# Where one branch of the first gate tile is projected: in the gate stage, or among the last attention blocks

## The chip, the cores and the metric

The kernel runs on one core of a Trainium2 chip. The core has a matrix engine (TensorE, PE in the profile, with its weight loads as PEld), a vector engine (VectorE, DVE), a scalar engine (ScalarE, ACT), a general engine (GpSimd, POOL) and a queue that issues most DMAs (SyncE, SP). Each engine works through its own instructions in order and waits on semaphores for the others. The metric is the device time of one execution in microseconds (us), with all inputs in device memory.

## The reference

One decoder block over a sequence of 1024 tokens of width 1024. A row norm is followed by a wide projection `w_in`; its columns give a forgetting attention (8 heads of 64), a differential attention (4 heads with two maps of 64 each), a SiLU factor z for both, and 2 x 1024 gate columns.

```python
h = rms_norm(x, g_pre[l], NORM_EPS)
proj = jnp.einsum('bsd,dn->bsn', h, w_in[l])
qa, ka, va, fa, za, qb, kb, vb, zb, gates = jnp.split(proj, SPLIT_POINTS, axis=-1)
...
ya = merge_heads(ya) * jax.nn.silu(za)
...
yb = merge_heads(yb) * jax.nn.silu(zb)
gate_a, gate_b = jnp.split(jax.nn.sigmoid(gates), N_BRANCHES, axis=-1)
merged = (gate_a * jnp.einsum('bsw,wd->bsd', ya, w_branch[l, 0])
          + gate_b * jnp.einsum('bsw,wd->bsd', yb, w_branch[l, 1]))
y = jnp.einsum('bsd,de->bse', merged, w_out[l])
x = x + rms_norm(y, g_post[l], NORM_EPS)
```

## The kernel before

All matrix operands are float32, cut in a high part (cast to float32r) and a low part (the difference). A product of two such operands is three matmuls: high by high, high by low, low by high. So each weight tile needs two instructions before PE can use it (`load_w`, L277): one for `hi`, one for `lo`; its arguments choose the engines.

The work goes in stages. First the transposed, normed input h^T is made (`hT`, 8 buffers) and the values are projected. Then come eight attention units, `u` = 0 to 7 (L642): 0 to 3 differential, 4 to 7 forgetting. While unit u attends, PE is given "filler": the q and k projections of unit u + 1 and some z projections, whose results are stored to device memory (`spill_tasks`, L383: load a weight tile, then two chunks of 512 tokens, 24 matmuls each into `ps`, copied by ACT to `zs` and stored). Unit 7 has no next unit; its filler is z6 and z7 alone.

A forgetting unit has two heads, m = 0 and 1, and takes 256 query rows at a time, block g = 3 down to 0. For each (g, m): scores (`s_row`, tiles Sf, two matmuls per piece), a minimum and bias on DVE, the exponential on ACT, a reciprocal on DVE and a scaling on POOL. The products of the block before are made meanwhile (`av`, L464): PE transposes 128 x 128 pieces of the softmax rows into a PSUM tile (`ptf`, L481, two buffers), ACT casts it (`phf`, L484), DVE subtracts (`plf`, L485), PE multiplies with V into one PSUM tile (`ypf`, L505, one buffer), and ACT and DVE take it out (`yt` L587, `ys` L588) for a store to `y_d`. The loop L661 to L673 emits, for each of the eight blocks n of a unit, its scores, then the products of the block before, then the filler that is due. The order on each engine is not the order in which the code is written: a scheduler sets it with a timeline of its own, within the dependences.

The gate stage (L802 to L850) makes gate tile d = 0 with the plain product (`gates_plain`: both branches, two chunks each, 96 matmuls, `pg`), and tiles d = 1 to 7 in pairs of branches with seven products in place of eight (`gates_pair`, `wino`, tiles x_g; 12 matmuls each). The seven products are numbered 1 to 7; 1, 2 and 3 use h^T itself, 4, 6, 5 and 7 use combinations of h^T that were stored earlier and are loaded here as eight tiles of 1 MB (`h_load`, T4 to T7, in buffers that attention held). The left operands a1 to a7 come from the two raw weight tiles by sums on POOL (S1 to S4) and a split on ACT and DVE or POOL, and take the buffers of `hi` and `lo` in turn with a third pair. `GATE` (L842) is the order of the products. Gates go through a sigmoid on ACT and are stored in `g_d`. `y_load` loads attention's results, `y_work` multiplies them by SiLU(z); `YORD` says after which tile.

Then y is cast to y^T (`yT`, high on ACT, low on DVE, L867 and L868), the branch products follow (`branch`, tiles pb, weights `br` by `load_w` with the high part on ACT and the low part on POOL, L899), each multiplied by its gate (`merge`), and the output product with its norm ends the kernel.

Of the kernel before, what the change touches and what calls it, by code (L numbers as in the profile page):

```python
# [32 lines left out]
        ((0, 0), (0, 1), (1, 0)), ((1, 1), (2, 0), (2, 1)), ((3, 0), (3, 1)), ())  # L33
ZFILL = ((0,), (1,), (), (2,), (3,), (4,), (5,), (6, 7))
# [13 lines left out]
def tile_hybrid_block(  # L48
# [58 lines left out]
    g_d = [[dram.tile([P, S], F32, name=f"g_d{d}_{b}") for b in range(2)] for d in range(KT)]  # L107
    ss_d = dram.tile([4, S], F32, name="ss_d")
# [194 lines left out]
    with ExitStack() as st:  # L303
# [135 lines left out]
        lastx, vload = [None], []  # L439

        def s_row(T, m, i, X, bias, boff, nm, le=None):

            A, B = (T["TA"], T["KA"]) if m == 0 else (T["TB"], T["KB"])
            n = (i + 1) * P
            qs = slice(i * P, (i + 1) * P)
            xs = slice(i % 2 * P, (i % 2 + 1) * P)
            pr = pp.tile([P, S], F32, tag="P", name=f"P{nm}_{m}_{i}")
            mx = small.tile([P, 2], F32, tag="mx", name=f"mx{nm}_{m}_{i}", bufs=8)
            pcs = pieces(i)
            for j, (a, b) in enumerate(pcs):  # L450
                ps = sps.tile([P, CH], F32, tag="S", name=f"S{nm}_{m}_{i}_{j}")[:, 0:b - a]
                nc.tensor.matmul(ps, lhsT=A[:, qs], rhs=B[:, a:b], start=True, stop=False)  # L452
                nc.tensor.matmul(ps, lhsT=X[:, xs], rhs=B[:, a:b], start=False, stop=True)  # L453
                nc.vector.tensor_tensor_reduce(  # L454
                    out=pr[:, a:b], in0=ps, in1=bias[:, boff + a:boff + b], scale=-0.125,
                    scalar=BIG if j == 0 else mx[:, j - 1:j], op0=ALU.add, op1=ALU.min,
                    accum_out=mx[:, j:j + 1])
            if le is None:
                le = small.tile([P, 1], F32, tag="l", name=f"l{nm}_{m}_{i}", bufs=8)
            nc.scalar.activation(pr[:, 0:n], pr[:, 0:n], AF.Exp,  # L460
                                 bias=mx[:, len(pcs) - 1:len(pcs)], scale=-1.0, accum_out=le)
            return pr, le
# [173 lines left out]

        T, tasks = unit_proj(0)
# [4 lines left out]
        for u in range(8):  # L642
# [18 lines left out]
            for n, (wgt, rws, prd) in enumerate(groups):  # L661
# [9 lines left out]
                while nf < len(fill) and nf < len(fill) * done / total:  # L671
                    fill[nf]()
                    nf += 1  # L673
        pend()
# [108 lines left out]
    def y_load(t):  # L783

        g = t // 2
        if t % 2 == 0:
# [22 lines left out]
    def gates_plain(d):  # L809
        for br in range(2):  # L810
            wt = load_w(f"g{br}_{d}", w_cols(GT + br * D + d * P), True, True)
            for c in range(2):
# [7 lines left out]

    def h_load():
# [3 lines left out]
        for m in (4, 6, 5, 7):  # L825
            for part in range(2):
                nc.sync.dma_start(f32(ts[m][part]), t_d[m][:, part])
            h_ops[m] = [[t[:, k, :] for k in range(4)] for t in ts[m]]

    def gates_pair(d, order):  # L830
        raw = []
        for br in range(2):
            r = wpool.tile([P, KT, P], F32, tag="wraw", name=f"raw{d}_{br}")
            nc.sync.dma_start(r, w_cols(GT + br * D + d * P))
            raw.append(r)
# [6 lines left out]
    GATE = (1, 2, 4, 6, 5, 7, 3)  # L842
    h_load()
    gates_plain(0)
    for t in (4, 5, 6, 7, 0, 1, 2, 3):
        y_load(t)
    for d in range(1, KT):
        gates_pair(d, GATE if d < KT - 1 else (7, 5, 6, 4, 1, 2, 3))
# [13 lines left out]

    yT = {}
# [32 lines left out]
    for br in range(2):  # L896
        for d in range(KT):
            if d % 2 == 0:
                wbr = load_w(f"br{br}_{d}", None, True, True, [  # L899
                    (slice(4 * n, 4 * n + 4),  # L900
                     wb[br][:, (d + n) * P:(d + n + 1) * P].rearrange("(k p) n -> p k n", p=P))
                    for n in range(2)])
# [178 lines left out]
```

## Time and profile before

| | us |
|---|---|
| median of three runs | 911.37 (909.87 to 914.45) |
| the profiled execution | 909.96 |
| its span, first to last instruction | 908.1 |
| PE busy in the span | 884.7 |
| mean granted clock of PE | 0.998 of full |

The span is what the profile's columns of time count in; the 1.9 us between the span and the execution's own time lie around it. A row of a group reads: line, engine, operation, output and input names, shape, count, then busy time and mean length, then the idle time ahead of it and who ended it. A row of the timeline starts with the start and the length in us. The unit boundaries in this execution: the scores and blocks of unit 7 end at 579.75, the plain gate projections run from there to 601.6, the pairs of gate tiles to 736.3, then the branches.

### The profile page before, as it was taken

What the parts mean: (1) busy time and instruction counts of PE and PEld (TensorE: products, weight loads), DVE (VectorE), ACT (ScalarE), POOL (GpSimd) and SP (SyncE); (2) the same over time, 40 slices, a digit from 0 to 9 for tenths busy, and PEclk for the clock granted to TensorE, in tenths of its full rate; (3) what the DMA queues carried; (4) which work ended last, traced back from release to release, by engine and by line L of the source; (5) the groups of instructions that cost most, each with busy time, mean ns of one, the idle gap of its engine ahead of it and who ended that gap; (6) DMA issues with size and microseconds to landing.
All of it is one profiled execution on the core that took longest, in us unless ns stands there. A gap on an engine that the chain in (4) does not pass through costs nothing.

```text
span 908.1 us, 13652 instructions
## 1 busy us (share of the span) xinstructions
PE 884.7 (97%) x4600; PEld 746.4 (82%) x4600; DVE 606.3 (67%) x1133; ACT 441.6 (49%) x877; POOL 447.2 (49%) x429
## 2 busy tenths in 40 slices
PE   7999999999999999999999999999999999999996
PEld 5899988788888888888888887788888888888885
DVE  6767547878678575467648548415678895648796
ACT  3433226576658584365545648534444352314352
POOL 7325325546555455254434446418566532483961
PEclk9999999999999999999999999999999999999999
DMA  9556747434335260432523432496555599210495
GB/s 323 188 177 255 270 119 194 110 82 130 102 87 163 70 180 18 147 86 71 165 74 84 133 100 65 180 402 224 160 162 186 176 308 327 71 46 0 122 198 168
DMA packets 128648, 139.04 MB, mean 153 GB/s; under 512 B 10289, under 2 KB 96305, under 8 KB 127554
## 3 DMA queue, kind: packets, MB, share of 16 engines
q1 hardware_dynamic: 124210, 135.82, 47.6%
q0 software_dynamic: 4224, 2.10, 2.0%
q8 instruction: 36, 0.59, 0.3%
q14 instruction: 34, 0.28, 0.1%
q10 hardware_dynamic: 144, 0.26, 0.1%
HBM read 85.65 MB, written 37.81 MB: 136 GB/s over the span
## 4 chain that ended last, share of the span: by engine, by line
PE 82%; DVE 6%; issue 4%; POOL 3%; DMA 2%; ACT 2%; SPq 1%; POOLq 0%; DVEq 0%; ACTq 0%
PE x_g L744 15%; PE pb L878 10%; PE pv L197 9%; PE x_o L744 9%; PE pz L298 8%; PE pk L298 7%; PE pq L298 7%; PE ypf L505 3%; PE ptf L481 2%; PE pg L298 2%; PE ypd L505 2%; PE Sd L452 2%; PE ptd L481 1%; PE Sf L452 1%; PE Sd L453 1%
## 5 line engine op out<-in xcount | busy, mean ns | idle before, releaser
L197 PE MATMUL pv<-wvhi,hT 128*128 128x264 f32 (+2 forms) x384 | 88.8, 323 | 0.4 <-DVE hT L183 0.4
L298 PE MATMUL pz<-hT,hi_z 128*128 128x512 f32 x256 | 83.3, 397 | 0.2 <-ACT sq L410 0.2
L298 PE MATMUL pk<-hT,hi_k 128*128 128x512 f32 x256 | 82.3, 395 | 0.9 <-DVE KB L351 0.9
L298 PE MATMUL pq<-hT,hi_q 128*128 128x512 f32 x256 | 81.7, 393 | 0.0
L878 PE MATMUL pb<-yT,hi_br 128*128 128x512 f32 x256 | 78.4, 389 | 0.0
L744 PE MATMUL x_g<-T,a_g 128*128 128x512 f32 x336 | 78.1, 391 | 0.0
L744 PE MATMUL x_o<-wo_op,a_o 128*128 128x512 f32 x336 | 77.6, 392 | 0.0
L744 PEld LDWEIGHTS x_o<-wo_op,a_o 128*128 128x128 f32 x336 | 63.0, 188 | 14.5 <-DVE a_o L694 0.5
L744 PEld LDWEIGHTS x_g<-T,a_g 128*128 128x128 f32 x336 | 63.1, 188 | 13.9
L197 PEld LDWEIGHTS pv<-wvhi,hT 128*128 128x128 f32 x384 | 64.2, 189 | 6.1 <-DVE hT L183 0.7
L460 ACT ACTIVATE Pd<-Pd,mxd 128x128 f32<-128x128 f32 (+7 forms) x64 | 49.7, 777 | 35.5 <-DVE mxd L454 35.1
L197 PE MATMUL pv<-wvlo,hT 128*128 128x512 f32 (+2 forms) x192 | 62.0, 325 | 0.7 <-DVE wvlo L153 0.7
L573 POOL TENSOR_TENSOR cb<-cb,trim 128x128 f32<-128x128 f32 x64 | 30.3, 477 | 65.7 <-DVE mxf L454 44.1
L485 DVE TENSOR_TENSOR plf<-ptf,phf 128x512 fp32r<-128x512 f32 (+1 forms) x80 | 50.0, 635 | 18.1 <-ACT phf L484 17.2
L547 POOL TENSOR_SCALAR Pd<-Pd,l,nlam 128x128 f32<-128x128 f32 (+7 forms) x32 | 29.3, 916 | 66.4 <-DVE l L546 60.2
L578 POOL TENSOR_SCALAR Pf<-Pf,lf 128x1024 f32<-128x1024 f32 (+3 forms) x64 | 47.9, 753 | 27.6 <-DVE lf L577 24.5
L460 ACT ACTIVATE Pf<-Pf,mxf 128x1024 f32<-128x1024 f32 (+3 forms) x64 | 49.9, 779 | 20.5 <-DVE mxf L454 19.7
L744 PE MATMUL x_g<-hT,a_g 128*128 128x512 f32 x252 | 59.0, 391 | 0.0
L878 PEld LDWEIGHTS pb<-yT,hi_br 128*128 128x128 f32 x256 | 48.0, 188 | 9.9
L744 PEld LDWEIGHTS x_g<-hT,a_g 128*128 128x128 f32 x252 | 47.3, 188 | 10.4
L298 PEld LDWEIGHTS pk<-hT,hi_k 128*128 128x128 f32 x256 | 47.2, 188 | 10.3 <-DVE KB L351 1.5
L298 PEld LDWEIGHTS pq<-hT,hi_q 128*128 128x128 f32 x256 | 47.6, 188 | 9.2
(253 smaller groups left out, 2366.1 us busy)
## 6 DMA issues: line engine op xcount, KB each, us to landing
t_d<-t SPq DMA_DIRECT2D x16, 512.0 KB, 4.2
T<-t_d SPq DMA_DIRECT2D x8, 1024.0 KB, 17.7
raw<-in_w_in_dram SPq DMA_DIRECT2D x14, 512.0 KB, 5.2
vb_d<-vbs SPq DMA_DIRECT2D x8, 512.0 KB, 3.8
va_d<-vas SPq DMA_DIRECT2D x8, 512.0 KB, 5.2
raw_k<-in_w_in_dram SPq DMA_DIRECT2D x8, 512.0 KB, 4.5
raw_q<-in_w_in_dram SPq DMA_DIRECT2D x8, 512.0 KB, 4.3
V<-vb_d SPq DMA_DIRECT2D x4, 1024.0 KB
```

The costliest lines, as they stand in the source:

```text
L197: nc.tensor.matmul(ps[n], lhsT=hT[hp][k // 4][i // 4][:, k % 4, hs], rhs=wt[k][:, a:b], start=first, stop=(k == KT - 1 and hp == 1))
L298: nc.tensor.matmul(ps, lhsT=a[:, k, :], rhs=hT[h][k // 4][c][:, k % 4, :], start=(k == 0 and a is hi and h == 0), stop=(k == KT - 1 and a ...
L452: nc.tensor.matmul(ps, lhsT=A[:, qs], rhs=B[:, a:b], start=True, stop=False)
L460: nc.scalar.activation(pr[:, 0:n], pr[:, 0:n], AF.Exp, bias=mx[:, len(pcs) - 1:len(pcs)], scale=-1.0, accum_out=le)
L481: nc.tensor.transpose(pt[:, o * P:(o + 1) * P], rows[2 * g + r][:, j * P:(j + 1) * P], ident)
L485: nc.vector.tensor_tensor(pl[:, 0:n], pt[:, 0:n], ph[:, 0:n], op=ALU.subtract)
L505: nc.tensor.matmul(o, lhsT=a, rhs=b[:, src], start=(j == 0 and n == 0), stop=(odd == 1 and jj == g and n == len(prods) - 1))
L547: nc.gpsimd.tensor_scalar(p2[:, 0:n], p2[:, 0:n], l2, nlam, op0=ALU.mult, op1=ALU.mult)
L573: nc.gpsimd.tensor_tensor(diag, diag, trim, op=ALU.add)
L578: nc.gpsimd.tensor_scalar(p1[:, 0:n], p1[:, 0:n], l1, 1.0, op0=ALU.mult, op1=ALU.mult)
L744: nc.tensor.matmul(x[m], lhsT=a[:, ai, k, :], rhs=right[m][bi][k], start=(k == 0 and n == 0), stop=(k == 3 and n == 2))
L878: nc.tensor.matmul(ps, lhsT=a[:, kk, :], rhs=yT[g][h][:, k % 2, sl], start=(k == 0 and a is hi and h == 0), stop=(k == 3 and a is lo))
```

## The change

It has five parts.

1. The first branch of gate tile 0 becomes a spilled projection, `gate`, of the form that z has: its weights are split on POOL and DVE, its two chunks are emitted in unit 7 after blocks n = 5 and n = 7 (`GFILL`), each behind the last score matmul of that block (`issue_after` orders it there on PE; `lasts` is that matmul), and stored to `gl_d`. `gates_plain` keeps the second branch alone, 48 matmuls in place of 96. After pair d = 2 the stored projection is loaded, goes through the sigmoid and is stored with the other gates.
2. The weights of the second branch are loaded ahead of the eight loads of T, and the raw weights of pair 1 are issued behind T4 in the code.
3. Pair 1 takes the products in the order 1, 2, 3, 4, 6, 5, 7: first those that need no T.
4. The loads of y are no longer issued together behind the plain projections, but each ahead of the pair after which it is used, behind that pair's raw weights on SP.
5. The first branch weight tile (`first`) is emitted ahead of the casts of y^T.

```diff
+GFILL = (5, 7)
...
-                nc.tensor.matmul(ps, lhsT=X[:, xs], rhs=B[:, a:b], start=False, stop=True)
+                lasts[0] = nc.tensor.matmul(
+                    ps, lhsT=X[:, xs], rhs=B[:, a:b], start=False, stop=True).ins
...
+        gate = spill_tasks("gl", GT, gl_d)
         T, tasks = unit_proj(0)
...
                     fill[nf]()
                     nf += 1
+                if u == 7 and n in GFILL:
+                    with tc.issue_after(lasts[0]):
+                        gate[GFILL.index(n)]()
...
     def gates_plain(d):
-        for br in range(2):
+        for br in (1,):
             wt = load_w(f"g{br}_{d}", w_cols(GT + br * D + d * P), True, True)
+            yield
...
+    def gate_raw(d):
+        raws[d] = []
+        for br in range(2):
+            r = wpool.tile([P, KT, P], F32, tag="wraw", name=f"raw{d}_{br}")
+            lastraw[0] = nc.sync.dma_start(r, w_cols(GT + br * D + d * P)).ins
+            raws[d].append(r)
...
+            if m == 4:
+                gate_raw(1)
...
+    plain = gates_plain(0)
+    next(plain)
     h_load()
-    gates_plain(0)
-    for t in (4, 5, 6, 7, 0, 1, 2, 3):
-        y_load(t)
+    run_all(plain)
     for d in range(1, KT):
-        gates_pair(d, GATE if d < KT - 1 else (7, 5, 6, 4, 1, 2, 3))
+        if d not in raws:
+            gate_raw(d)
+        with tc.issue_after(lastraw[0]):
+            for t, c in YORD[d]:
+                if c == 0:
+                    y_load(t)
+        gates_pair(d, (1, 2, 3, 4, 6, 5, 7) if d == 1 else GATE if d < KT - 1 else (7, 5, 6, 4, 1, 2, 3))
+        if d == 2:
+            for c in range(2):
+                g = tmp.tile([P, CH], F32, tag="t", name=f"g0_0_{c}")
+                nc.sync.dma_start(g, gl_d[:, c * CH:(c + 1) * CH])
+                gate_out(0, 0, c, g, g)
...
+    first = branch_w(0, 0)
     yT = {}
...
-                wbr = load_w(f"br{br}_{d}", None, True, True, [
-                    (slice(4 * n, 4 * n + 4),
-                     wb[br][:, (d + n) * P:(d + n + 1) * P].rearrange("(k p) n -> p k n", p=P))
-                    for n in range(2)])
+                wbr = first if br == d == 0 else branch_w(br, d)
```

On PE, near the end of unit 7 before, at the last scores (block 0 of head 1, Sf_1_0) and the transposes and products of blocks 2 and 1 (the digits after the name are head, block and piece, then a buffer number):

```order
L453 MATMUL Sf_1_0_0_6713<-KB_5341,X1f_0_6697 128x128
L505 MATMUL ypf_1_2_6515<-plf_1_2_2_6540,V_5848 128x256
L505 MATMUL ypf_1_2_6515<-phf_1_2_2_6539,V_5848 128x128
L505 MATMUL ypf_1_2_6515<-plf_1_2_2_6540,V_5848 128x128
L481 MATMUL ptf_0_1_1_6621<-ident,Pf_0_2_6505 128x128
```

The same place in the changed kernel (pgl is the moved projection; of a row of its matmuls the first ones are shown):

```order
L455 MATMUL Sf_1_0_0_6748<-KB_5342,X1f_0_6732 128x128
L300 MATMUL pgl_6773<-hT_91,hi_gl 128x512
L300 MATMUL pgl_6773<-hT_95,hi_gl 128x512
L300 MATMUL pgl_6773<-hT_91,lo_gl 128x512
...
L508 MATMUL ypf_1_2_6516<-plf_1_2_2_6541,V_5849 128x256
L508 MATMUL ypf_1_2_6516<-phf_1_2_2_6540,V_5849 128x128
L508 MATMUL ypf_1_2_6516<-plf_1_2_2_6541,V_5849 128x128
L484 MATMUL ptf_0_1_1_6622<-ident,Pf_0_2_6506 128x128
```

Between the last scores and the products that followed them stand 15 of the second chunk's 24 matmuls; 3 and 6 more stand behind the next two groups of transposes, and the last of them directly ahead of the first product of block 1. The first chunk stands likewise, 19 and 5, behind the scores of head 1's block 1 and behind the next two groups of transposes of head 0's block 2; the group of transposes ptf_1_2_2 (head 1, block 2) has none between it and those ahead of it.

On ACT, before, the end of unit 7 (yt takes a product out, phf casts a transposed block, the ACTIVATE is an exponential):

```order
L460 ACTIVATE Pf_1_0_6711,lf_1_0_6717<-Pf_1_0_6711,mxf_1_0_6712 128x128
L587 COPY yt_0_1_6638<-ypf_0_1_6611 64x256
L484 CAST phf_1_1_1_6677<-ptf_1_1_1_6676 128x384
L484 CAST phf_0_0_0_6723<-ptf_0_0_0_6722 128x384
L587 COPY yt_1_1_6692<-ypf_1_1_6666 64x256
```

And in the changed kernel (a_g are the left operands a1 and a2 of pair 1, sgl is the copy of the second chunk):

```order
L463 ACTIVATE Pf_1_0_6746,lf_1_0_6752<-Pf_1_0_6746,mxf_1_0_6747 128x128
L700 CAST a_g_6926<-raw_0_6858 128x512
L395 COPY sgl_6798<-pgl_6773 128x512
L700 CAST a_g_6944<-raw_0_6858 128x512
L590 COPY yt_0_1_6639<-ypf_0_1_6612 64x256
L487 CAST phf_1_1_1_6712<-ptf_1_1_1_6711 128x384
```

The two casts and the copy now stand between the last exponential and the copy yt; before, the casts of pair 1 stood behind the last phf of the unit and later.

On ACT at the passage to the branches, in the changed kernel; before, the cast of hi_br stood behind the two rows of yT from yf:

```order
L809 ACTIVATE zs_1_7906<-zs_1_7906 128x512
L286 CAST hi_br_0_8066<-raw_br_0_8063 128x1024
L900 CAST yT_2_8070<-yf_6924 128x1024 x2
L900 CAST yT_3_8076<-yf_7082 128x1024 x2
L754 COPY c_g_8004<-x_g_7991 128x512
```

More of the change, by code (lines that the diff above doesn't have):

```diff
@@ L107, in tile_hybrid_block @@
     g_d = [[dram.tile([P, S], F32, name=f"g_d{d}_{b}") for b in range(2)] for d in range(KT)]
+    gl_d = dram.tile([P, S], F32, name="gl_d")
     ss_d = dram.tile([4, S], F32, name="ss_d")
@@ L437, in swapped @@
             return t
-        lastx, vload = [None], []
+        lastx, vload, lasts = [None], [], [None]
         def s_row(T, m, i, X, bias, boff, nm, le=None):
@@ L785, in y_load @@
         g = t // 2
-        if t % 2 == 0:
+        if g not in yz:
             if t < 4:
@@ L819, in tile_hybrid_block @@
              for m, (kh, sh) in hB.items()}
+    raws, lastraw = {}, [None]
+    def gate_raw(d):
[4 more added lines that the diff above has]
+            raws[d].append(r)
     def h_load():
@@ L827, in h_load @@
                 nc.sync.dma_start(f32(ts[m][part]), t_d[m][:, part])
+            if m == 4:
+                gate_raw(1)
             h_ops[m] = [[t[:, k, :] for k in range(4)] for t in ts[m]]
     def gates_pair(d, order):
[L831 to L835, printed above, removed]
+        raw = raws[d]
         left = left_operands(f"g{d}", raw[0][:, 0:4], raw[0][:, 4:8], raw[1][:, 0:4], raw[1][:, 4:8])
@@ L861, in slot, with branch_w @@
         return s[0].tile(shape, dtype, tag=s[1], name=name)
+    def branch_w(br, d):
+        return load_w(f"br{br}_{d}", None, True, True, [
+            (slice(4 * n, 4 * n + 4),
+             wb[br][:, (d + n) * P:(d + n + 1) * P].rearrange("(k p) n -> p k n", p=P))
+            for n in range(2)])
+    first = branch_w(0, 0)
     yT = {}
```

## The prediction

> **What bounds it now.** The page comes first: which engine is full over the whole span.
>
> ```profile
> span 908.1 us, 13652 instructions
> PE 884.7 (97%) x4600; PEld 746.4 (82%) x4600; DVE 606.3 (67%) x1133; ACT 441.6 (49%) x877; POOL 447.2 (49%) x429
> ```
>
> PE (TensorE) is busy for 884.7 of 908.1 us. The change leaves PE's matmuls as many as they were, so it can win only from time in which PE stands still, and that is 23.4 us by this row. Next, busy time by stretch shows where: a piece of unit 7, the end of unit 7 cut in three, the plain gate projections, the first pair of gate tiles, the passage from gates to branches.
>
> ```profile
> core 0: us, PE busy (x) PEld busy (x) DVE busy (x) ACT busy (x) POOL busy (x), PEclk, DMA share, GB/s
> 528.90:549.00 20.10, 20.10 (x113) 17.27 (x111) 10.35 (x31) 11.62 (x23) 8.30 (x12) 1.00 0.34 106
> 549.00:563.41 14.41, 13.79 (x96) 11.76 (x95) 12.56 (x39) 11.44 (x24) 10.12 (x13) 1.00 0.27 75
> 563.41:574.37 10.96, 8.93 (x66) 7.41 (x65) 8.72 (x29) 8.85 (x25) 5.30 (x11) 1.00 0.04 13
> 574.37:579.75 5.38, 4.70 (x33) 3.92 (x34) 3.99 (x12) 4.18 (x12) 2.63 (x5) 1.00 0.12 38
> 579.75:601.60 21.85, 21.85 (x98) 18.07 (x98) 2.54 (x4) 5.11 (x9) 6.10 (x5) 1.00 0.99 395
> 601.60:620.60 19.00, 19.00 (x85) 15.59 (x83) 7.15 (x10) 6.47 (x11) 7.57 (x6) 1.00 1.04 378
> 725.00:750.00 25.00, 25.00 (x112) 20.61 (x111) 23.93 (x23) 14.03 (x18) 8.18 (x4) 1.00 0.93 313
> ```
>
> Until 549 the filler of unit 7 (the z projections) keeps PE full; from 601.60 on it is full too, also at the passage at 725 to 750. The hole is between 549 and 579.75, once the filler is used up and only softmax blocks are left. The waits of PE from 545 to 580 say for whom:
>
> ```profile
> PE ptf L481 <- DVE plf L485: 1.7, 4, 0.7
> PE ypf L505 <- DVE plf L485: 0.7, 3, 0.3
> PE ypf L505 <- ACT phf L484: 0.3, 1, 0.3
> PE ypf L505 <- DVE ys L588: 0.2, 1, 0.2
> ```
>
> Every one is a link of one block's chain: PE transposes a softmax block (pt), ACT casts it (ph), DVE takes the rest (pl), PE multiplies (yp), ACT and DVE take out the product (yt, ys). In 563.41 to 574.37 DVE and ACT are busy for 8.72 and 8.85 of 10.96 us, so neither is full; PE waits for their delay, not for their throughput, and other PE work in the gap would hide it.
>
> **How much PE stands still.** The busy column counts each matmul's modelled end, so I also go by starts. Two neighbours, a wait, and the marks of the last stretch, in PE's timeline:
>
> ```profile
> 565.82 0.28 PE L505 MATMUL ypf<-plf,V 128*128 128x256 f32 x1
> 565.94 0.28 PE L505 MATMUL ypf<-phf,V 128*128 128x256 f32 x1
> ...
> 568.24 0.62 PE L481 MATMUL ptf<-ident,Pf 128*128 128x128 f32 x4
> 568.62 0.36 PE L452 MATMUL Sf<-KB,TB 128*128 128x256 f32 x1
> 568.82 0.28 PE L453 MATMUL Sf<-KB,X1f 128*128 128x256 f32 x1
> 569.81 0.55 PE L481 MATMUL ptf<-ident,Pf 128*128 128x128 f32 x3 [0.71 <-DVE plf L485]
> ...
> 574.37 0.39 PE L505 MATMUL ypf<-phf,V 128*128 128x256 f32 x1
> ...
> 576.54 0.38 PE L505 MATMUL ypf<-phf,V 128*128 128x256 f32 x1
> ```
>
> A product of 256 columns takes 0.12 us from start to start, four transposes take 0.38, so 0.095 each. The groups of that window by line give what stands in 563.41 to 579.75:
>
> ```profile
> L505 PE MATMUL ypf<-plf,V 128*128 128x256 f32 (+1 forms) x26 | 6.8, 301 | 0.4 <-DVE plf L485 0.4
> L505 PE MATMUL ypf<-phf,V 128*128 128x256 f32 (+1 forms) x25 | 6.6, 288 | 0.7 <-ACT phf L484 0.3 <-DVE ys L588 0.2
> L481 PE MATMUL ptf<-ident,Pf 128*128 128x128 f32 x38 | 6.2, 280 | 1.6 <-DVE plf L485 1.5
> ```
>
> That is 51 products and 38 transposes; with the 9 score matmuls, 60 x 0.12 + 38 x 0.095 = 10.8 us of work in 16.34 us: 5.5 us of stall by starts, against (10.96 - 8.93) + (5.38 - 4.70) = 2.7 us by the busy column. The starts count what a filler could use, so I go by 5.5 and keep 2.7 as the low end. The last stretch holds 33 of the 98, 24 x 0.12 + 9 x 0.095 = 3.7 us of work, so 1.7 us of the stall lies there and 3.8 us ahead of it.
>
> **The change, part by part.**
>
> *The 48 matmuls that move.* The plain stretch holds 96 of them in 21.85 us, 0.228 each: 48 are 10.9 us. They leave the plain stretch, where PE is full, and stand between the softmax blocks, 24 behind the scores of block 1 (in place of 563.41) and 24 in four pieces up to the row at 574.37. PE's work stays the same; the stalls that they cover are the gain. In the order, one group of transposes still has nothing ahead of it: the one at 569.81, started 0.99 us after a matmul of 0.12. I leave its 0.87 standing and count the rest of the first stretch as covered: 3.8 - 0.9 = 2.9 us gained. Ends: 2.0 (the busy column's idle time there) and 3.8.
>
> *The last stretch.* No filler stands behind the row at 574.37, but three new instructions stand on ACT there, ahead of the copy yt: the cast of a1 (it waits for the last of the 48, whose weight buffer it takes), the copy of the second result, the cast of a2. What ACT and DVE do there now, and the nearest rows for the new ones:
>
> ```profile
> 540.43 0.59 ACT L393 COPY sz<-pz 128x512 f32<-128x512 f32 x1 [0.21 <-PE pz L298]
> ...
> 575.66 0.37 ACT L587 COPY yt<-ypf 64x256 f32<-64x256 f32 x1
> 576.06 0.95 ACT L484 CAST phf<-ptf 128x384 fp32r<-128x384 f32 x2
> ...
> 578.61 0.62 ACT L693 CAST a_g<-raw 128x512 fp32r<-128x512 f32 x1
> ```
>
> The three take 0.62 + 0.59 + 0.62 = 1.8 us, 1.7 with the overlap of neighbours. They start when the last of the 48 ends, which is when the row at 574.37 would start; so yt starts 1.7 us behind it, not 575.66 - 574.37 = 1.3. Behind yt are queued ph of the next two blocks, and for ys, behind yt, waits the product at 576.54. So the stretch grows by 0.4 us. Ends: nothing (ACT has the slack) and 1.7 (all three on the path).
>
> *Sum.* 2.9 - 0.4 = 2.5 us gained; from 2.0 - 1.7 = 0.3 to 3.8.
>
> *The filler ahead of it.* Four z matmuls of 0.228 stand earlier in PE's order and score rows later. That stretch (549 to 563.41) idles 0.6 us; I take nothing, between 0.6 won and 0.9 lost. The split of the moved weights goes from ACT and POOL to POOL and DVE, at about 530, where PE is full with filler; without that cover DVE's 1.2 us (a quarter of the row of four, 4.63, below) would be on the path.
>
> *The T tiles.* The first product of pair 1 now starts 10.9 us earlier against attention's end. In its place:
>
> ```profile
> 579.10 1.36 SPq L827 DMA_DIRECT2D T<-t_d  x3
> 581.42 3.42 SPq L827 DMA_DIRECT2D T<-t_d  x5
> DMA to landing us min/median/max: 17.7/17.7/17.7
> ...
> 601.61 5.61 PE L744 MATMUL x_g<-hT,a_g 128*128 128x512 f32 x24
> 607.06 11.20 PE L744 MATMUL x_g<-T,a_g 128*128 128x512 f32 x48
> ```
>
> PE needed T4 27.3 us after attention's end (607.06 - 579.75). Now it needs it after 48 plain matmuls and three products of 12, 84 x 0.228 = 19.1 us, and T6, T5, T7 at steps of 2.7 (T7 at 27.3). The new order (products 1, 2, 3 first) buys back one product. Eight loads of 1.05 MB at 395 GB/s take 21.2 us from 579.10; the landing shown, 17.7 us, counted from the last issue (under 584.84), gives 602.5, 22.8 us behind attention's end. In the order of issue T4 is through after a quarter, 5 us, and T7 at 22.8, each 4 us or more early: nothing lost. The loads of y, 4.2 MB that stood in the same stream, go behind the raws. The stored branch comes back in pair 2: 1 MB both ways, 2.7 us at that rate, for which only a sigmoid waits.
>
> *The branch weights.* hi_br now goes ahead of four casts of y^T:
>
> ```profile
> 728.92 3.89 ACT L867 CAST yT<-yf 128x1024 fp32r<-128x1024 f32 x4
> 732.72 1.05 ACT L284 CAST hi_br<-raw_br 128x1024 fp32r<-128x1024 f32 x1
> 729.99 4.63 DVE L868 TENSOR_TENSOR yT<-yf,yT 128x1024 fp32r<-128x1024 f32 x4 [0.25 <-ACT yT L867]
> 735.23 2.75 DVE L868 TENSOR_TENSOR yT<-yd,yT 128x1024 fp32r<-128x1024 f32 x1
> 733.84 3.05 POOL L288 TENSOR_TENSOR lo_br<-raw_br,hi_br 128x1024 fp32r<-128x1024 f32 x1 [5.50 <-ACT hi_br L284]
> 736.28 1.52 PE L878 MATMUL pb<-yT,hi_br 128*128 128x512 f32 x6
> ```
>
> PE is full here, so nothing is won. The risk: lo_br, on POOL, now runs beside DVE's first differences. In these rows the one beside it took 2.75 us, not 4.63 / 4 = 1.16. If the four start only when POOL is through (728.92 + 1.05 + 3.05 = 733.0), the last ends at 737.7; the first branch product needs it as its eleventh matmul, 736.28 + 10 x 0.228 = 738.6. Cost nothing; without those 0.9 us each us late is a us. The Trainium skill, SBUF — State Buffer, section Who interferes with whom, speaks against this move: a VectorE instruction with two SBUF inputs and a GpSimd one that reads SBUF shut each other out for the whole instruction. The 2.75 us agrees with it; by it the last difference comes at 737.7, without it at 735.7, and the sum is the same.
>
> **The number.** The profiled execution took 909.96 us, its span 908.1, so 1.9 lie around it, and it is 1.4 under the median of the runs, 911.37. Span 908.1 - 2.5 = 905.6; the execution 907.5; the median 908.9.
>
> **Rivals.**
>
> *All of it is covered* (no wait left in the first stretch, and the filler lets DVE and ACT run so far ahead that the last stretch shrinks too): 5.5 us, 905.9. For it: DVE is free during 10.9 us of filler. Against: the last blocks' chains start only after the filler. Chance 0.14.
>
> *The wait moves to ACT.* ACT's queue is in order; a1 waits for PE while ph of two blocks stand behind it. All 1.7 us on the path: 2.9 - 1.7 = 1.2 won, 910.2. Against: in the order the blocks ahead of a1 are already cast. Chance 0.2.
>
> *It does not do what it says.* The chains are so short that PE finds the same stalls behind each piece of filler: 911.4. For it: no wait in the rows above is longer than 0.7 us, a link's delay, which filler elsewhere does not shorten. Chance 0.11.
>
> *The T tiles come late* (the other side). If the eight loads share the rate and end together at 22.8 us, x4 waits from 19.1: 3.7 lost, 2.5 won, 912.6. It decides from 21.6 us on, and each further us costs one. For it: only one landing is shown. Against: PE never showed a wait for T. The Trainium skill, DMA: Bandwidth & Descriptors, section Queues, rings and completion order, has each DMA engine take descriptors in ring order, by which T4 lands first; no row here shows it. Chance 0.07.
>
> *The forecast*: 0.48.
>
> **From cases to numbers.** A measurement of this kernel can tell about 0.5% from no change, 4.6 us here. Only the first rival (0.14) and a little of the forecast's upper tail reach below 906.8: faster 0.16. Slower by 4.6 us needs the T tiles at over 26 us: 0.03. The rest, 0.81, is within. The range leaves out half of the first rival and most of the T case: 905.9 to 911.9.
>
> **What would show it.** Right: PE's idle time from the scores of block 1 to the plain projections falls by some 2 us, the wait of pt for pl shrinks to one of about 0.7, the plain stretch is 10.9 us, and PE stays full behind it. Wrong: PE waiting for a DMA at the first x_g with T, for a_g in pair 1, or for yT or lo_br at the first pb; or yp waiting for ys for over 1 us near the end of unit 7.

## The result, and the profile after

The changed kernel takes 909.17 us, median of 20 runs (906.92 to 912.46), beside 911.33 of the kernel before (20 runs, 909.34 to 914.62): ratio 0.9975, 95% interval 0.9965 to 0.9985, which leaves out 1. That is 2.2 us less. The profiled execution took 907.85 us, its span is 906.1, against 909.96 and 908.1.

The page of the changed kernel: PE has the same work, so what was won is time in which it stood still.

```profile
span 906.1 us, 13659 instructions
PE 884.7 (98%) x4600; PEld 746.8 (82%) x4600; DVE 604.5 (67%) x1134; ACT 439.2 (48%) x878; POOL 445.5 (49%) x429
```

Busy time by stretch (start and end, length, then PE, PEld, DVE, ACT and POOL, each with its number of instructions, then the granted clock of PE, the share and the rate of the DMA engines), cut at the same places of the work: the first stretch of attention's end, now with the moved matmuls in it; the last stretch; the plain projections; the passage from gates to branches.

```profile
563.20:582.37 19.17, 18.70 (x114) 16.25 (x113) 10.14 (x33) 10.57 (x30) 6.11 (x12) 1.00 0.08 28
582.37:588.07 5.70, 4.41 (x34) 3.82 (x33) 3.77 (x9) 4.03 (x9) 4.25 (x5) 1.00 0.18 62
588.07:599.02 10.95, 10.95 (x51) 9.07 (x51) 2.15 (x4) 3.42 (x6) 2.46 (x2) 1.00 0.98 376
...
725.00:750.00 25.00, 24.89 (x108) 19.77 (x107) 23.07 (x24) 14.43 (x18) 8.34 (x4) 1.00 1.00 346
```

The first stretch holds 10.9 us more work (48 x 0.228) and is 8.2 us longer: 2.7 won. The last one is 5.70 us, not 5.38: 0.3 lost. The plain stretch is half of what it was. The last row is new: at the passage from gates to branches PE, full before, idles.

The waits of PE at attention's end (us in total, times, longest):

```profile
PE ypf L508 <- DVE ys L591: 0.8, 1, 0.8
PE ptf L484 <- DVE plf L488: 0.7, 2, 0.5
```

The longest wait for pl, in PE's timeline:

```profile
572.60 0.28 PE L455 MATMUL Sf<-KB,X1f 128*128 128x256 f32 x1
573.34 0.55 PE L484 MATMUL ptf<-ident,Pf 128*128 128x128 f32 x3 [0.47 <-DVE plf L488]
```

Four waits of pt for pl, 1.7 us, have become two, 0.7 us. The one shown is the one that the order left without a matmul ahead of it: 0.74 us from start to start, less 0.12 of work, so 0.62 us; the forecast left 0.87 standing. ACT's timeline at the start of the last stretch:

```profile
582.34 0.62 ACT L700 CAST a_g<-raw 128x512 fp32r<-128x512 f32 x1
582.86 0.58 ACT L395 COPY sgl<-pgl 128x512 f32<-128x512 f32 x1
583.34 0.62 ACT L700 CAST a_g<-raw 128x512 fp32r<-128x512 f32 x1
583.98 0.37 ACT L590 COPY yt<-ypf 64x256 f32<-64x256 f32 x1
```

PE's timeline in the same stretch:

```profile
582.37 0.28 PE L508 MATMUL ypf<-phf,V 128*128 128x256 f32 x1
...
584.85 0.39 PE L508 MATMUL ypf<-phf,V 128*128 128x256 f32 x1 [0.77 <-DVE ys L591]
```

The three new instructions stand ahead of yt, which starts 1.61 us behind PE's row at 582.37 (forecast 1.7). Behind yt comes ys, and PE waits 0.77 us for that.

**The passage.** The chain that ended last in the changed kernel (start, length, what) no longer runs through PE alone. It comes from the side engines, as I call DVE, ACT and POOL with the loads for them:

```profile
717.45 5.32 DMA zs<-z_d
...
726.88 1.68 POOL yd L808
728.56 0.02 issue
728.58 0.02 ACT zs L809
...
729.12 1.04 ACT hi_br L286
730.16 0.95 ACT yT L900
731.11 0.02 issue
731.13 0.98 DVE yT L901
732.12 1.53 issue
733.65 1.22 DVE yT L901
734.87 0.04 issue
734.91 86.77 PE pb L911 x380
```

PE begins the branches at 733.72, not 736.28, and finds the second low part of y^T not yet there:

```profile
733.72 0.62 PE L911 MATMUL pb<-yT,hi_br 128*128 128x512 f32 x2
734.18 0.40 PE L911 MATMUL pb<-yT,lo_br 128*128 128x512 f32 x1
734.42 1.00 PE L911 MATMUL pb<-yT,hi_br 128*128 128x512 f32 x2
735.26 0.40 PE L911 MATMUL pb<-yT,lo_br 128*128 128x512 f32 x1
```

The last two take 0.84 us from start to start, where the first two take 0.46. A second, smaller gap follows the matmul at 744.85: the next one, the first of the third output tile, starts 0.38 us behind it, not 0.23. The likely reason is the PSUM buffer that it takes over: DVE's addition cu_g, which still reads a product of pair 7 out of PSUM, ends at 745.09, 0.14 us ahead of that start.

**One table for all kernels.** The last projection of unit 7 (pq) starts anywhere between 486.90 and 491.57 us in the profiled executions, although nothing ahead of it was edited: what comes before it differs by up to 4.7 us from execution to execution. So I count from that matmul, in four stages: to the first product of pair 1, to the first branch product, to the first output product, to the end. The marks of the changed kernel, in PE's timeline:

```profile
486.90 0.39 PE L300 MATMUL pq<-hT,lo_q 128*128 128x512 f32 x1
...
599.02 8.40 PE L751 MATMUL x_g<-hT,a_g 128*128 128x512 f32 x36
...
821.52 1.32 PE L751 MATMUL x_o<-wo_op,a_o 128*128 128x512 f32 x5
```

```
profiled execution, us     to pair 1    pairs   branches   output      sum
before                        114.52   134.67      87.05    84.82   421.06
changed                       112.12   134.70      87.80    84.55   419.17
e1 weights behind             112.09   134.72      88.77    84.56   420.14
e2 low part on DVE            112.15   134.70      87.10    84.58   418.53
e3 y one pair earlier         112.19   136.23      87.05    84.54   420.01
e4 gate early                 112.85   137.24      89.13    84.55   423.77
e5 old pair order             112.17   134.71      87.05    84.53   418.46
e6 third piece                112.36   136.02      88.60    84.90   421.88
e6 and low part on DVE        112.39   136.11      87.05    84.90   420.45
e7 old order, casts last      111.65   134.75      87.88    84.58   418.86
e8 third piece, ACT/POOL      111.46   136.22      87.20    84.89   419.77
e9 weights first in before    114.50   134.67      87.04    84.81   421.02
e10 y loads together          112.18   143.22      88.89    84.54   428.83
e10 three together            111.60   134.74      87.05    84.55   417.94
```

Attention's end gives 2.40 us, the passage takes back 0.75, and 0.27 come in the output stage. These 0.27 lie behind the start of DVE's last two instructions (903.47 to 908.15 before, 901.66 to 906.07 in the changed kernel), and I have no cause for them. The first two stages repeat to a tenth of a us where nothing in them was edited. The branches don't: how full they are depends on where the side engines are when PE arrives. Medians, with the spread ahead of the mark in them, can't part versions that lie half a us apart.

### The profile page after: what moved, and what is told of

Its sections match the earlier page's. It is cut to its first block, busy times and chain, and to the rows that moved or that the text cites. A ratio compares the mean times of both kernels' runs of the same rounds, so it can differ in the third digit from the quotient of the medians.

```text
span 906.1 us, 13659 instructions
## 1 busy us (share of the span) xinstructions
PE 884.7 (98%) x4600; PEld 746.8 (82%) x4600; DVE 604.5 (67%) x1134; ACT 439.2 (48%) x878; POOL 445.5 (49%) x429
```

## The experiments

**Who holds PE at the passage.** My theory (A): the chain of zs, yd, hi_br and the first differences of y^T comes too late for a PE that arrives 2.56 us earlier. First the last part of the change undone:

```diff
-    first = branch_w(0, 0)
...
-                wbr = first if br == d == 0 else branch_w(br, d)
+                wbr = branch_w(br, d)
```

> The changed kernel with its last part alone undone: the first branch weights are cast behind the four casts of y^T again. Theory A (the side engines reach the passage at their own clock time: the last zs load at 717.45, the last sigmoid of ACT at 728.58, whatever PE does, and PE now comes 2.56 us earlier): hi_br ends at about 734.1, the low part at 736.9 as before, PE has six high products to do from 734.1 and then waits from 735.5 to about 736.9. The passage loses about 1.5 to 2.1 us instead of 0.75, the span is 906.9 to 907.5. Theory B (putting the weights ahead of the casts is itself what costs the 0.75 us): the loss goes, the span is 905.4.

Measured: the median is 910.33 us, 0.9987 of before (0.9975 to 0.9998). PE's timeline:

```profile
734.64 1.10 PE L910 MATMUL pb<-yT,hi_br 128*128 128x512 f32 x4
735.95 0.73 PE L910 MATMUL pb<-yT,hi_br 128*128 128x512 f32 x2 [0.21 <-DVE cu_g L744]
737.59 0.50 PE L910 MATMUL pb<-yT,lo_br 128*128 128x512 f32 x1 [0.91 <-POOL lo_br L290]
```

The branches take 88.77, 1.7 us over the full 87.05, where theory A has 1.5 to 2.1; theory B falls. The weights ahead of the casts save about 1 us here (88.77 - 87.80). In the kernel before they should save nothing; the same edit put into that one:

> The kernel before with the changed kernel's last part alone: the first branch weights ahead of the casts of y^T. Theory A (in the kernel before PE reaches the branches 2.6 us later against the side engines, so all of it is hidden): first branch product to first output product 87.05 us as before, from the last projection of unit 7 to the end 421.0. Rival (weights ahead and POOL's work beside DVE cost PE 0.5 us or more by themselves): 87.5 or more.

Measured: 911.58 us, 1.0002 (0.9985 to 1.0018); every stage as before to 0.03 us, though the first differences of y^T stretch there as well. DVE's timeline of that kernel:

```profile
732.73 6.00 DVE L875 TENSOR_TENSOR yT<-yf,yT 128x1024 fp32r<-128x1024 f32 x4 [1.20 <-ACT yT L874]
```

So the stretched differences cost something only where PE comes early. What stretches them: in the changed kernel DVE's first difference took 2.59 us, beside lo_br on POOL. DVE's timeline, then POOL's:

```profile
731.13 2.59 DVE L901 TENSOR_TENSOR yT<-yf,yT 128x1024 fp32r<-128x1024 f32 x1 [1.19 <-ACT yT L900]
```

```profile
730.23 2.41 POOL L290 TENSOR_TENSOR lo_br<-raw_br,hi_br 128x1024 fp32r<-128x1024 f32 x1 [1.69 <-ACT hi_br L286]
```

POOL is through at 732.64, the difference 1.08 us behind that: about what one takes alone. The Trainium skill, SBUF — State Buffer, section Who interferes with whom, has it that DVE's second port is POOL's and is held exclusively; the rows agree. The test moves the low part to DVE:

```diff
-    def branch_w(br, d):
-        return load_w(f"br{br}_{d}", None, True, True, [
+    def branch_w(br, d, lo_pool=True):
+        return load_w(f"br{br}_{d}", None, True, lo_pool, [
...
-    first = branch_w(0, 0)
+    first = branch_w(0, 0, False)
```

> The changed kernel with the low part of the first branch weights computed on DVE instead of POOL; the high part stays ahead of the casts. Theory A with its second half (the first difference of y^T took 2.59 us instead of 1.21 because POOL's lo_br ran beside it, and that is the last link before PE): lo_br takes DVE some 1.2 us ahead of the differences, these take 1.21 each, the second is done by about 733.8 where PE needs it at 734.6, and PE also finds its PSUM buffer free at the third output block; the 0.75 us of the passage comes back, span 905.4. Rival (the work beside it is harmless, only the queue's length counts): DVE has 1.2 us more in its queue, the second difference ends at about the same 734.9, span 906.1 or a little above.

Measured: 908.99 us, 0.9972 (0.9959 to 0.9985). DVE's timeline:

```profile
731.44 1.23 DVE L290 TENSOR_TENSOR lo_br<-raw_br,hi_br 128x1024 fp32r<-128x1024 f32 x1 [0.24 <-ACT hi_br L286]
732.58 4.63 DVE L901 TENSOR_TENSOR yT<-yf,yT 128x1024 fp32r<-128x1024 f32 x4
```

DVE has one instruction more, and the five together take 5.8 us where four took 6.0. The branches take 87.10 instead of 87.80, and the sum falls by 0.64: theory A, second half included. That this is the edit's doing shows best at the same lag: in the changed kernel and in e8 below PE starts the branches 5.14 us behind the start of the last sigmoid of y, and they take 87.80 with the low part on POOL, 87.20 with it on DVE (e8 has a third piece of filler besides). A longer lag does it too: at 6.0 us the passage is full with the low part on POOL (e5 below). The other way to give room, the products of y a pair earlier:

```diff
-YORD = ((), ((4, 0), (4, 1)), ((5, 0), (5, 1), (6, 0)), ((6, 1), (7, 0), (7, 1)),
-        ((0, 0), (0, 1), (1, 0)), ((1, 1), (2, 0), (2, 1)), ((3, 0), (3, 1)), ())
+YORD = ((), ((4, 0), (4, 1), (5, 0)), ((5, 1), (6, 0), (6, 1)), ((7, 0), (7, 1), (0, 0)),
+        ((0, 1), (1, 0), (1, 1)), ((2, 0), (2, 1), (3, 0), (3, 1)), (), ())
```

> The changed kernel with the products of y, z and the sigmoid spread over pairs 1 to 5 (3, 3, 3, 3, 4 pieces) instead of 1 to 6 (2, 3, 3, 3, 3, 2), so that none is left for the last two pairs. Theory A: ACT, DVE and POOL are through with y long before the passage, the high part of the weights follows its load, the casts of y^T come several us earlier, PE waits for nothing at the branches: 0.75 us won, span 905.4, if pair 6 and 7 do not wait for their own operands. Rival (PE is slower at the passage for another reason, for example beside so many reads of SBUF): span 906.1.

Measured: 911.83 us, 0.999 (0.9975 to 1.0005). The passage is full (87.05), as forecast, but the pairs lose 1.5 us. PE's timeline in pair 7:

```profile
722.96 8.40 PE L751 MATMUL x_g<-T,a_g 128*128 128x512 f32 x34 [0.55 <-DVE a_g L701]
```

My condition "if pair 6 and 7 do not wait for their own operands" was not met: four pieces of y ahead of pair 7 delay its own operands. The room moved, it did not grow.

**Where the room went.** Between the first product of pair 1 and POOL's first sum of pair 2 lie 11.7 us in the kernel before (613.30 - 601.61) and 18.7 in the changed one (617.67 - 599.02), and in both POOL had waited for the raw weights. POOL's timeline of before, then of the changed kernel:

```profile
613.30 1.29 POOL L706 TENSOR_TENSOR S_g<-raw 128x512 f32<-128x512 f32 x1 [1.27 <-DMA raw<-in_w_in_dram]
```

```profile
617.67 1.29 POOL L713 TENSOR_TENSOR S_g<-raw 128x512 f32<-128x512 f32 x1 [2.33 <-DMA raw<-in_w_in_dram]
```

Pair by pair the side engines catch up; at pair 7 POOL's lag against PE is 2.7 us (701.75 - 599.02 against 701.67 - 601.61). But 2.4 us of that are PE's own gain. Counted from the mark of the table, 487.09 and 486.90, POOL comes to pair 7 only 0.3 us later than before (214.85 against 214.58 us). The last sigmoid of y on ACT, before and changed:

```profile
728.38 0.64 ACT L802 ACTIVATE zs<-zs 128x512 f32<-128x512 f32 x1 [1.66 <-POOL yd L801]
728.58 0.64 ACT L809 ACTIVATE zs<-zs 128x512 f32<-128x512 f32 x1 [1.67 <-POOL yd L808]
```

That is 241.29 and 241.68 us behind the mark; in e9, e1 and e2 it is 241.85, 241.22 and 241.54. In all kernels whose pairs lose nothing it lies between 240.5 and 241.9, while PE's first product of pair 1 lies between 111.6 and 114.5; where PE waits in the pairs it is later, 242.5 and more (e3, which moves y itself, aside). So the side engines come to the passage at the place that they had, to 0.4 us, while PE comes 2.4 us earlier: theory A, counted from the mark. What paces the side engines until then is not shown.

At pair 2 they are 4.6 us late by the mark (130.77 against 126.21). About half of that comes with the new order of pair 1, as e5 shows below. The likely cause of the rest, which no run parts, is that the loads for the pairs now have 10.95 us of plain projections to land in, not 21.85. How much hangs on those loads shows the next kernel, with the loads of y together as before:

```diff
     run_all(plain)
+    for t in (4, 5, 6, 7, 0, 1, 2, 3):
+        y_load(t)
...
-        with tc.issue_after(lastraw[0]):
-            for t, c in YORD[d]:
-                if c == 0:
-                    y_load(t)
```

> The changed kernel with the eight loads of y in one group ahead of pair 1, as in the kernel before, instead of one or two ahead of each pair. Theory A (the side loop is paced by itself, by the two raw buffers and the queue of POOL): raws, sums and sigmoids come at the same distance from attention's end as in the changed kernel, the passage loses 0.75 us, 419.2 from the last projection of unit 7 to the end. Theory C (the loads of y, now among the raws, are what holds the side engines back by 2.8 us against PE): the last sigmoid of y comes up to 2.8 us earlier, the passage loses nothing, 418.5.

Measured: 919.38 us, 1.0086 (1.0066 to 1.0107). Neither theory holds. PE's timeline in pair 2:

```profile
631.79 0.73 PE L751 MATMUL x_g<-T,a_g 128*128 128x512 f32 x2 [3.10 <-ACT a_g L700]
633.73 12.30 PE L751 MATMUL x_g<-T,a_g 128*128 128x512 f32 x46 [1.20 <-POOL a_g L701]
```

With 4.2 MB of y ahead of them, the second raw weights of pair 2 are issued 17.4 us behind the first product of pair 1, not 9.2; the pairs lose 8.5 us, and the passage takes 1.8. About 1.5 of the 8.5 us are no wait for an operand: behind the rows shown, PE's granted clock is 0.52 from 633.70 to 637.00, and matmuls there start 0.43 us apart instead of 0.23. In the kernel before, the loads of y stood together as well, and its pairs take 134.67. Without the loads one by one the change, with its order of pair 1, would have been 7.8 us slower than the kernel before, in stages.

**The order of pair 1.** It was changed for the T tiles. Undone:

```diff
-        gates_pair(d, (1, 2, 3, 4, 6, 5, 7) if d == 1 else GATE if d < KT - 1 else (7, 5, 6, 4, 1, 2, 3))
+        gates_pair(d, GATE if d < KT - 1 else (7, 5, 6, 4, 1, 2, 3))
```

> The changed kernel with the products of pair 1 in the order before (1, 2, 4, 6, 5, 7, 3), so that T4 is needed 2.7 us earlier, 36 - 12 = 24 plain-sized matmuls behind the first product, 5.4 us. Counted in stages, since the start of the last projection of unit 7 differs by up to 4 us from execution to execution. Theory (the T tiles were never late: the first lands some 10 us after its issue): no wait of PE for T, first product of pair 1 to first branch product 134.7 us as in the changed kernel. Rival (the eight T loads share the rate and end together 22.8 us behind attention's end): PE waits some 6 us at T4, the stage takes 140 us.

Measured: 908.88 us, 0.9977 (0.9963 to 0.9992). PE has no wait for T: the new order was not needed. It has a price of its own at pair 2: with it the second raw weights of that pair are issued 9.2 us behind the first product of pair 1, with the old order 1.4 us ahead of it, and POOL's first sum of pair 2 comes 18.7 us behind that product, with the old order 16.4 (16.3 and 16.5 in e7 and the last kernel below). The passage is full here, since PE reaches the branches 6.0 us behind the last sigmoid, not 5.1. But with the same order e7 below has 5.0 and the last kernel 5.9, so one execution does not tell what the order is worth at the passage.

**What the filler is.** The moved projection behind the scores of blocks 0 and 1:

```diff
-GFILL = (5, 7)
+GFILL = (0, 1)
```

> The changed kernel with the moved projection behind the scores of blocks 0 and 1 of unit 7 instead of 5 and 7; the z projections that fill PE there stay where they are in the code. Theory (the gain is cover for the chain of the last blocks, which have no other filler): PE is full at blocks 0 and 1 anyway, the last blocks find their stalls again, so the end of attention comes 10.9 us later than in the kernel before and the gain of 2.6 us at it is gone; the passage then costs nothing either, since PE comes to it as late as before. Span about 908.1. Rival (the gain comes from the loads of T and the raws in their new order, or from the shorter plain stretch): span stays near 906.1.

Measured: 913.27 us, 1.0026 (1.0015 to 1.0037). It did not tell the two theories apart as meant: with the gate ahead of them in the queue, the z projections slid into the gap. PE's timeline:

```profile
572.91 0.39 PE L300 MATMUL pz<-hT,lo_z 128*128 128x512 f32 x1
```

Their last matmul starts at 572.91, not 548 as before and in the changed kernel, and the stage to pair 1 keeps 1.7 of the 2.4 us: the cover is worth its time whatever is computed under it. That the gain comes with the filler and not with the other parts, the other kernels say: attention's end keeps 2.34 to 2.43 us of gain with part 5 (e1), part 3 (e5) or part 4 (the loads of y together) undone. Part 2 was not undone by itself; but the plain stretch, which it serves, had no idle time to give (21.85 us busy of 21.85 before). Pairs and passage lose 3.9 us against the changed kernel, waiting for a_g and yT; why the side engines come later still I did not find.

**More filler.** A third piece, the first half of the second branch of gate tile 0, behind the second; its result goes by DRAM as that of the first branch does:

```diff
+        more = spill_tasks("gr", GT + D, gr_d, rbox)
...
                         gate[GFILL.index(n)]()
+                        if n == 7:
+                            more[0]()
...
-            wt = load_w(f"g{br}_{d}", w_cols(GT + br * D + d * P), True, True)
+            wt = rbox[0]
             yield
-            for c in range(2):
+            for c in (1,):
```

> The changed kernel with a third piece of 24 matmuls moved: the first half of the second branch of gate tile 0, which the order puts between the last two blocks. Theory A (cover): the 2 us of stall by starts in the last stretch shrink by 1.0 to 1.5 us, so from the last projection of unit 7 to the first product of pair 1 the time falls from 112.1 to about 110.9; nothing for T is late by more than 0.7. Theory A's second half (the side engines' loop of load, sum, cast and difference runs at 20 to 21 us a pair against PE's 19.0, so PE's lead at the passage is what is left): what is won ahead of the passage is lost at it; first branch product to first output product grows from 87.8 to 88.4 to 89.0 us, and from the last projection of unit 7 to the end it is 419.2 as before or at best 0.3 less. Rival (a gain at attention's end carries through): 418.0.

> The third piece and the low part of the first branch weights on DVE together. Theory A: the second edit gives the passage about 1 us of room, so the gain of the third piece is kept up to that; from the last projection of unit 7 to the end 417.5 to 418.0 us (the changed kernel 419.2, with the low part on DVE alone 418.5). Rival (the two share one gain): 418.5.

Measured: 911.83 us, 1.001 (0.9994 to 1.0027), and 911.02, 1.0 (0.9986 to 1.0014). Both miss: the stage to pair 1 is 0.24 us longer, not 1.2 shorter. The last stretch did shrink, by 0.7 us, but 0.9 went ahead of it. DVE's timeline there, then PE's at that place and in pair 1:

```profile
550.14 1.77 DVE L291 TENSOR_TENSOR lo_gr<-raw_gr,hi_gr 128x1024 fp32r<-128x1024 f32 x1
551.94 0.42 DVE L593 TENSOR_TENSOR ys<-ypf,yt 64x256 f32<-64x256 f32 x1
```

```profile
552.41 0.39 PE L510 MATMUL ypf<-phf,V 128*128 128x256 f32 x1 [1.00 <-DVE ys L593]
...
617.23 2.81 PE L756 MATMUL x_g<-T,a_g 128*128 128x512 f32 x11 [0.99 <-DMA T<-t_d]
```

The new filler's own weights are subtracted on DVE at 550.14, where the z filler has just ended; ys and PE wait behind it. And T7, 24.3 us behind the first T issue (592.89), is now late by 1 us. If the first is right, the weights on ACT and POOL mend it:

```diff
-                        box[0] = load_w(nm, w_cols(c0))
+                        box[0] = load_w(nm, w_cols(c0), nm == "gr", nm == "gr")
```

> The third piece and the low part of the first branch weights on DVE, as before, but the third piece's own weights cast on ACT and subtracted on POOL, as the plain projection's are, not on POOL and DVE. Theory (the 0.92 us that the third piece lost ahead of the first moved matmul is DVE's difference of its weights, 1.77 us at 550.1, on the path since the z filler has ended): the last projection of unit 7 to the first moved matmul takes 76.3 us again instead of 77.2, to the first product of pair 1 111.4 to 111.6 instead of 112.4; PE still waits about 1 us for T7, so the end comes after 419.4 to 419.7 us. Rival (the third piece itself makes the blocks later): 77.2 stays.

Measured: 910.60 us, 0.9989 (0.9974 to 1.0004). The way to the first moved matmul is 76.30 us again, the stage to pair 1 111.46, 0.7 under the changed kernel; T7 is late by 1.2 us, and the sum is 0.6 above the changed kernel's. More filler is limited by the T loads, whose cover it takes.

**The last stretch.** The old order of pair 1, and a1 and a2 cast behind the last yt (`lasty` is that copy):

```diff
-                        nc.scalar.copy(tmp[64:128], yp[64:128])
+                        lasty[0] = nc.scalar.copy(tmp[64:128], yp[64:128]).ins
...
-            split(t, v, nc.gpsimd if m in (2, 4) and nm not in ("o2", "o3") else nc.vector)
+            with tc.issue_after(lasty[0]) if nm == "g1" else ExitStack():
+                split(t, v, nc.gpsimd if m in (2, 4) and nm not in ("o2", "o3") else nc.vector)
```

> The changed kernel with the old order of products in pair 1 and, beside it, the casts of a1 and a2 of pair 1 queued on ACT behind the last copy yt of attention. Theory (a1 and a2 stand ahead of yt and ph of the last two blocks and cost 0.3 us there): the copy of the second moved result stays ahead, yt starts about 0.6 us behind the last moved matmul instead of 1.6, though for its product only after its own 0.9 us, so the last stretch shrinks from 5.70 to 5.0 to 5.4 us; pair 1 still finds a1 and a2 ready, 10 us ahead. From the last projection of unit 7 to the first product of pair 1 111.5 to 111.85 instead of 112.15, to the end 417.8 to 418.1 (with the old order alone 418.4). Rival (ACT has the slack, the chain of the last block is as long without them): 5.70, 418.4; or the casts come too late for pair 1, a wait of PE for a_g at its first product.

Measured: 910.05 us, 0.9974 (0.9959 to 0.9989). ACT's timeline, then PE's:

```profile
585.27 0.59 ACT L396 COPY sgl<-pgl 128x512 f32<-128x512 f32 x1 [0.36 <-PE pgl L300]
586.20 0.37 ACT L591 COPY yt<-ypf 64x256 f32<-64x256 f32 x1 [0.34 <-PE ypf L509]
```

```profile
587.07 0.39 PE L509 MATMUL ypf<-phf,V 128*128 128x256 f32 x1 [0.28 <-DVE ys L592]
```

The wait for ys falls from 0.77 to 0.28 us, the last stretch from 5.70 to 5.21 (585.07 to 590.28): as forecast. But the passage then loses 0.83 us, not the 0 that I took over from e5, so the sum, 418.86, misses the 417.8 to 418.1. With the low part on DVE as well:

> The changed kernel with the old order of products in pair 1, the casts of a1 and a2 behind the last copy yt, and the low part of the first branch weights on DVE. Theory A: attention's end keeps the 0.5 us of the second edit (111.65 us from the last projection of unit 7 to the first product of pair 1), and the third gives the passage its room back (87.05 to 87.1 instead of 87.88); to the end 418.0 to 418.2 instead of 419.2, the median about 1 us under the changed kernel's. Rival (what is won at attention's end goes at the passage whatever stands there): 418.5 to 418.9.

Measured: 909.27 us, 0.998 (0.9966 to 0.9994). In stages it takes 417.94, 3.1 us under the kernel before and 1.2 under the changed one, the least of all, and just under the forecast of 418.0 to 418.2; the medians do not part it from the changed kernel, beside which it did not run. Its passage is full (87.05), but PE comes there 5.9 us behind the last sigmoid, close to the 6.0 of e5, whose passage was full without the third edit. So how much the third edit gives here is not shown.

## Why the prediction came out, step by step

- *First stretch: 2.9 won.* It is 2.7, and the wait that was to stay stayed (0.62 us of the 0.87). Busy time and starts had given ends of 2.0 and 3.8: more was won than the busy column showed as idle, and starts were the better count.
- *Last stretch: 0.4 lost.* It is 0.3, by the mechanism given: three ACT instructions ahead of yt. e7 takes two of them away and wins 0.5, so they cost a little more than the lengthening showed. The rival with all 1.7 us on the path falls.
- *The filler ahead of it: nothing.* From the last projection to the first moved matmul it is 76.30 us, to the same place before 76.32. The clause "without that cover DVE's 1.2 us would be on the path" was shown by e6 and e8: in e6 the difference, 1.77 us long, was on it, for 0.9, and e8, without it on DVE, has the 0.9 back.
- *T tiles: nothing lost.* Right, and with the old order too. T7 lands 24.3 us behind the first issue (in e6); in the changed kernel, with the first issue at 587.42, that is an estimated 611.7, some 3.8 us ahead of its product at 615.50.
- *The branch weights: "Cost nothing; without those 0.9 us each us late is a us."* This step failed. It set the side engines' 737.7 against PE's old arrival, 736.28, while the same sum sent PE there 2.5 us earlier. It also took the last low part, for the eleventh matmul, as the one that decides. In the order that ran, the last one is used by the fifteenth matmul, at 737.34, and is ready at 737.13; the one that decides is the second, for the fifth. Against 733.72 the wait was there to be read: the fifth matmul comes at 734.6 (733.72 + 4 x 0.228), the second low part, by the forecast's own figures, at 735.3 (733.0 + 2 x 1.16). The passage costs 0.75 us, and e1, e2, e8 and e9 show its parts: a PE that comes early, and a difference that waits for POOL. Putting the weights first was still right, by about 1 us.
- *Not in the forecast at all:* what the halved plain stretch and the new order of pair 1 do to the loads of the raw weights. I priced the shorter stretch for T alone. The side engines are 4.6 us late at pair 2 by the mark, half of that with the new order; by pair 7 it is 0.3 us, so it is not shown to cost anything in this kernel. With the loads of y together it costs 8.5 us in the pairs.
- *The number.* 2.5 forecast, 2.2 in the medians; in stages 2.40 - 0.03 - 0.75 + 0.27 = 1.9. That the total came out near the forecast with one of its steps wrong by 0.75 is luck: the 0.27 of the output stage, which no step named, and the spread ahead of the mark made up for part of it. The forecast also held that some 0.5% can be told from no change; these 20 and 20 runs told 0.25%. The rival *does not do what it says* falls with the first stretch, the rival *all of it is covered* with the waits that stay.

Open: the 0.27 us of the output stage, the worth of the pair order at the passage, what paces the side engines through the pairs, and the loss of e4's pairs.

## What to carry to other kernels

A gain ahead of a full stretch makes the full engine early everywhere behind it, so check every margin there against the new arrival, not the old. Filler is not free of cost: its own operands need an engine at a place that is still covered, and work taken from a stretch uncovers the loads that landed under it. Where the start of an execution varies more than the change is worth, count stages from a mark behind it.

## What the runs showed of the hardware

DVE's 128x1024 difference of two SBUF tiles takes 1.2 us alone and 2.59 beside a POOL subtraction of 2.41, ending 1.08 after it. In the kernel with the loads of y together, PE stands still for 3.10 and 1.20 us in pair 2, and behind that its granted clock is 0.52 for 3.3 us (633.70 to 637.00).

Eight T loads of 1.05 MB land in the order of issue, as far as the trace has it. In e6 it has three landings, of the loads issued first, fourth and last, at 592.89, 596.02 and 598.32; they took:

```profile
DMA to landing us min/median/max: 5.4/10.0/18.9
```

So they landed at 598.3, 606.1 and 617.2. The products with the first of them run on time from 607.59, and only the last, 24.3 us behind the first issue, is waited for. In the prediction I had no row for that. The Trainium skill, DMA: Bandwidth & Descriptors, section Queues, rings and completion order, has each DMA engine take the descriptors of a queue in ring order, and the three landings agree.
